# Moving the left-over weights of a mixture-of-experts router into the branch that uses them

## The chip, the cores and the metric

The kernel runs on one core of one Trainium2 chip. Its time is the device time of one execution in microseconds (us); below it is given as the median of several runs. The engines are PE (TensorE: matrix products), DVE (VectorE), ACT (ScalarE), POOL (GpSimd) and SP (SyncE, which here issues DMAs). A letter q behind an engine's name means its instruction sequencer: DMA issues, register loads, branches and semaphore waits. All times inside an execution are counted from its first instruction.

## What is computed

A decoder layer over 512 tokens and 16 meta tokens: attention and a state-space mixer in parallel, a gated merge, and then the part that the change touches, a hierarchical mixture of experts with 4 groups of 8 experts each.

```python
def hier_moe(v, w_group, b_group, w_expert, b_expert, w_gate, w_up, w_down):
    vt = v.reshape(-1, D_MODEL)                       # 512(+16) tokens x 1024
    g_logits = (vt @ w_group + b_group)
    p_group = jax.nn.softmax(g_logits, axis=-1)
    g_idx = jnp.argmax(g_logits, axis=-1)             # one group of 4
    p_g = jnp.take_along_axis(p_group, g_idx[:, None], axis=-1)
    e_logits = (vt @ w_expert + b_expert).reshape(-1, 4, 8)
    e_logits = jnp.take_along_axis(e_logits, g_idx[:, None, None], axis=1)[:, 0]
    top_vals, top_idx = lax.top_k(e_logits, 2)        # two experts of that group
    w = jax.nn.softmax(top_vals, axis=-1) * p_g
    ...
    for gi in range(N_EXPERT_GROUPS):                 # 32 experts, 1024 -> 256 -> 1024
        h = silu(einsum('td,edf->tef', vt, w_gate[sl])) * einsum('td,edf->tef', vt, w_up[sl])
        out = out + einsum('tef,te,efd->td', h, comb[:, sl], w_down[sl])
    return out.reshape(shp)
```

All is float32. The weights of the 32 experts are 3 MiB each: a gate and up table of 2 MiB (`gu`) and a down table of 1 MiB (`dn`).

## The kernel before

**Tokens and slots.** The 512 tokens are four blocks of 128 (b = 0 to 3). The kernel computes only chosen pairs: each expert has 64 slots (`CAP`), and a chosen token gets a slot by its rank among the tokens of that expert. A pass p of the expert loop takes two experts at once, 16 passes in all. A token whose rank is 64 or more, or whose group holds more than 256 tokens (`GCAP`), is left over: a general path (`tc.If(over > 0)`, line 1461) recomputes it with loops over all experts. The flag `ovi` is whether any expert has more than 64 tokens.

**The router**, lines 1354 to 1406, is written out by hand. PE follows the written order from line 1354 on; ACT, DVE and POOL follow it from line 1371 (`in_order`); the other engines' work and what stands outside is placed by a list scheduler at build time. For each block: `turn(b, hh)` adds the last projection to the residual, turns it on PE, sums its squares on ACT (`sqv`) and writes it to the DRAM table `vd`. `norm_v(b)` makes the factor of the norm (`ms` on DVE, a power on POOL) and writes it as a last column of `vd`. `logits` gives the router's products. `choose` is a generator of DVE steps (maximum, its index, the group's mask, the two best experts, the one-hot table `ohc`), cut up by `steps`. `rank` counts on PE, in the PSUM tile `rk`, how many earlier tokens chose the same expert; ACT copies the groups' ranks out (`rkg`, `rkf`). `find_slots` turns ranks to one-hot slot tables (`rr`). `weigh_exp` and `weigh` make the two weights, by an exponential on ACT. `place(b0, dst, v)` multiplies `rr` with the token numbers (v = 2, to `tb`) or with the weight table `vw` (v = 3, to `tw`): what comes out is, for every slot, its token or its weight. `idx` is `tb` as integers.

**What follows the router.** Three gathers on POOL (line 1431) fetch the rows of passes 0 to 2 from `vd` by `idx` into the tiles `xg`, which ACT has filled with zeros before (line 1422). Behind the gathers POOL sets `flag`, SP writes it to DRAM as `fence` (128 values of 4 bytes, line 1444), and only behind that issue SP loads the two halves of expert 4's `gu` (line 1445). `overflow` (line 1332) is for each of three block ranges 12 small steps on POOL that end in `wrest`, the weights of left-over tokens, and give `gk`, `bad` and `fine`, which the group tables need too. They too are placed behind the gathers. Then every engine loads `ovi` (line 1460) and branches around the general path (line 1461). Behind the branch SP issues the `dn` of experts 5 and 6 (line 1518) and then, in the expert loop, each next table as its buffer comes free: 7 `gu` buffers, 7 `dn` buffers.

**The expert loop**, from line 1696, keeps ACT, DVE, PE, POOL and SP in the written order: `turn_x` (turn the gathered rows on PE, `xT` on DVE), `expert_gu` (32 products, line 1554), activation, `expert_h`, the products with `dn` (line 1593), `combine` back to tokens, and a scatter of the finished rows after each group. `group_tables` (line 1633) runs on DVE once, in pass 0.

In these lines the order of the first steps is fixed:

```python
        norm_v(3)
        weigh(0)
        logits(3, 1)
        place(0, tb, 2)
        steps(c3, 10)
```

Of the kernel before, what the change touches and what calls it, by code (L numbers as in the profile page):

```python
# [73 lines left out]
def hybrid_layer(ctx: ExitStack, tc, A, out):  # L74
# [1052 lines left out]
    wrest = cp.tile([128, NE, 4], F32, name="wrest")  # L1127
# [7 lines left out]
    gk, bad, fine = (cp.tile([128, 4], F32, name=x) for x in ("gk", "bad", "fine"))  # L1135
# [14 lines left out]
    last_rs, last_sq = [None], [None]  # L1150

    def turn(b, hh, po=None):

        h = h2[:, b, hh * 512:(hh + 1) * 512]
        t = vT[b, hh] = gt("vbT", n=T, p=gr)
        pt = ps("pvT")
        two = b == 3 and hh
        for i in range(2):
            c = slice(i * 256, (i + 1) * 256)
            if po is not None and (two or i == 0):  # L1160
                o = c if two else slice(0, 512)
                dve.scalar_tensor_tensor(h[:, o], po[:, o], 0.5, h[:, o], op0=ALU.mult, op1=ALU.add)
            for k in (2 * i, 2 * i + 1):
                pe.transpose(pt[:, k * 128:(k + 1) * 128], h[:, k * 128:(k + 1) * 128], ident)
        last_sq[0] = act.activation(gt("sqv", n=T, p=gr), h, AF.Square, scale=2 * D ** -0.5, accum_out=vq[:, 2 * b + hh:2 * b + hh + 1])
        nc.sync.dma_start(vd[b * 128:(b + 1) * 128, hh * 512:(hh + 1) * 512], h)
        if two:
            return lambda: [dve.tensor_copy(t[:, i * 256:(i + 1) * 256], pt[:, i * 256:(i + 1) * 256]) for i in range(2)]
        elif hh:
            dve.tensor_copy(t, pt)  # L1170
        else:
            act.activation(t, pt, AF.Copy)
# [16 lines left out]
    def norm_v(b):  # L1189

        rs = vq[:, 8 + b:9 + b]
        t = sm.tile([128, 1], F32, tag="sq1", name="ms4", bufs=4)
        dve.tensor_scalar(t, vq[:, 2 * b:2 * b + 1], vq[:, 2 * b + 1:2 * b + 2], 4 * EPS, op0=ALU.add, op1=ALU.add)
        pool.tensor_tensor(rs, t, mhalf[:, :1], op=ALU.pow)
        q = nc.scalar if b < 3 else nc.sync
        last_rs[0] = q.dma_start(vd[b * 128:(b + 1) * 128, D:D + 1], rs)
# [3 lines left out]
    def choose(b0, b1):  # L1200
# [23 lines left out]
        vt_, vw, rr = rtile([2, 32]), rtile([4, 32]).rearrange("p b (k v) e -> p b k v e", k=2), rtile([2, 64])  # L1224
# [41 lines left out]
        chosen[b0] = b1, ak, vt_, vw, rtile([2]), rt_, rtile([2]), rr, rtile([2]), mx8, lg, gm, [rtile(n) for n in ([5], [5], [], [1], [1], [4])]  # L1266
# [10 lines left out]
    def weigh(b0):  # L1277

        b1, ak, vt_, vw, wk, rt_, rkk, rr, wx, mx8, lg, gm, (gd, eg, sg_, pg, e2, _) = chosen[b0]
# [52 lines left out]
    def overflow(b0):  # L1332

        b1, ak, vt_, vw, wk, rt_, rkk, rr, wx = chosen[b0][:9]
        g4_ = chosen[b0][12][5]
        pool.tensor_tensor(g4_, ohc[:, b0:b1, 32:], rkg[:, b0:b1], op=ALU.mult)
        pool.tensor_tensor(g4_[:, :, :2], g4_[:, :, :2], g4_[:, :, 2:], op=ALU.add)
        pool.tensor_tensor(gk[:, b0:b1], g4_[:, :, 0], g4_[:, :, 1], op=ALU.add)
        bd_ = bad[:, b0:b1]
        pool.tensor_scalar(wx, rkk, CAP - 0.5, None, op0=ALU.is_gt)  # L1340
        pool.tensor_scalar(bd_, gk[:, b0:b1], GCAP - 0.5, None, op0=ALU.is_gt)
        pool.tensor_tensor(bd_, bd_, wx[:, :, 0], op=ALU.add)
        pool.tensor_tensor(bd_, bd_, wx[:, :, 1], op=ALU.add)
        pool.tensor_scalar(fine[:, b0:b1], bd_, 0.5, None, op0=ALU.is_lt)
        pool.tensor_scalar(bd_, bd_, 0.5, None, op0=ALU.is_gt)
        pool.tensor_tensor(wx, wk, bd_[:, :, None].to_broadcast([128, b1 - b0, 2]), op=ALU.mult)
        pool.tensor_tensor(rt_, ak, wx[:, :, :, None].to_broadcast([128, b1 - b0, 2, 32]), op=ALU.mult)
        pool.tensor_tensor(wrest.rearrange("p e b -> p b e")[:, b0:b1], rt_[:, :, 0], rt_[:, :, 1], op=ALU.add)  # L1348
# [5 lines left out]
    with in_order(pe):  # L1354
# [18 lines left out]
        weigh_exp(0)  # L1373
        copies = turn(3, 1, po3)
        steps(c2)
        rank(2)
        copies()
        norm_v(3)
        weigh(0)
        logits(3, 1)  # L1380
        place(0, tb, 2)
        steps(c3, 10)
        weigh_exp(2)
        steps(c3)
# [9 lines left out]
        ovf, ovi = sm.tile([128, 1], F32, tag="sq1", name="ovf", bufs=4), cp.tile([128, 1], I32, name="ovi")  # L1394
        dve.tensor_reduce(ovf, rk[:, 144:176], axis=AX.X, op=ALU.max)
        dve.tensor_scalar(ovi, ovf, CAP + 0.5, None, op0=ALU.is_gt)
# [12 lines left out]

    n_traced = len(nc.cur_bb.bb.instructions)  # L1410
    overflow(0)
    overflow(2)
    overflow(3)
    overs = nc.cur_bb.bb.instructions[n_traced:]
# [216 lines left out]
    fst = cp.tile([128, 16], F32, name="fst")  # L1631

    def group_tables():
        goh = ohc[:, :, 32:]
        dve.tensor_scalar(fst, lpos, FIRST, None, op0=ALU.is_ge)
# [3 lines left out]
        dve.scalar_tensor_tensor(gtab[:, :, 0], goh, ic[:, 104:105], fine[:, :, None].to_broadcast([128, 4, 4]),  # L1639
# [250 lines left out]
```

## Time and profile before

| what | value |
|---|---|
| median of 3 runs | 827.81 us (826.03 to 828.17) |
| the profiled execution: its time | 824.92 us |
| its span, first to last instruction | 823.2 us |
| PE busy | 774.9 us, 94% |
| DVE, ACT, POOL busy | 454.9, 299.6, 147.5 us |
| moved by DMA | 163.39 MB, mean 198 GB/s |

The profiled execution is one of its own, 2.89 us under the median of the timed runs; what is added up inside it is counted against 824.92 us. PE's busy time counts pipelined products one by one, so 94% does not say that PE is at its limit. The page's row of DMA rates by slices is at about 420 GB/s from soon after the expert loop's start to near the end of the span, and at half of that or less in most slices before.

### The profile page before, as it was taken

To read this page: it belongs to the slowest core of one execution; us is meant where nothing else is said; L and a number is where in the kernel's file an instruction comes from. 1 tells how busy PE (TensorE), PEld (TensorE's weight loads), DVE (VectorE), ACT (ScalarE), POOL (GpSimd) and SP (SyncE) were. 2 spreads that over 40 slices of the span, in tenths; PEclk is the share of its full clock that TensorE was granted. 3 is DMA by queue.
4 is the path that set the end of the run, shared out by engine and by line. 5 is a ranking of instruction groups with operands and counts; after the bars stand their busy time and mean duration, and the time that the engine had idled before them with its cause. 6 is when DMAs were issued, how large, how long until landed. Compare 5 with 4: busy or idle time off the path is not lost.

```text
span 823.2 us, 11366 instructions
## 1 busy us (share of the span) xinstructions
PE 774.9 (94%) x4202; PEld 530.7 (64%) x4202; DVE 454.9 (55%) x1009; ACT 299.6 (36%) x564; POOL 147.5 (18%) x233
## 2 busy tenths in 40 slices
PE   4999999999999999999999899995699999999995
PEld 3999987677778878876666588884234343434342
DVE  3697528976356445477775775425243454543523
ACT  6455425333124374155554333412022322322313
POOL 5000103333112000023444300005300020200101
PEclk9999999999999999999999999997799999999998
DMA  7322226233231224021122595586799999999991
GB/s 254 109 61 97 103 67 203 92 126 129 78 111 56 103 86 155 14 62 31 44 53 66 159 423 194 175 333 204 153 422 421 419 418 420 417 420 418 420 386 40
DMA packets 40366, 163.39 MB, mean 198 GB/s; under 512 B 9152, under 2 KB 13648, under 8 KB 24176
## 3 DMA queue, kind: packets, MB, share of 16 engines
q1 hardware_dynamic: 35504, 154.46, 50.0%
q0 software_dynamic: 3984, 7.94, 3.0%
q8 instruction: 35, 0.57, 0.3%
q10 hardware_dynamic: 816, 0.20, 0.1%
q14 instruction: 27, 0.22, 0.1%
HBM read 159.30 MB, written 6.36 MB: 201 GB/s over the span
## 4 chain that ended last, share of the span: by engine, by line
PE 77%; DMA 8%; issue 5%; DVE 5%; ACT 3%; POOL 2%; POOLq 0%; SPq 0%; DVEq 0%; ACTq 0%
PE gu L1554 9%; DMA gu<-in_moe_gu_dram 5%; PE y L1593 5%; PE pbr L669 3%; PE pbr L672 3%; PE pbr L670 3%; PE pc L1620 2%; PE po L872 2%; PE ga L242 2%; PE gs L242 2%; PE ga L244 2%; PE ga L243 2%; PE gs L243 2%; PE gs L244 2%; PE pout L1094 2%
## 5 line engine op out<-in xcount | busy, mean ns | idle before, releaser
L1554 PE MATMUL gu<-gu,xT 128*64 128x512 f32 (+1 forms) x544 | 117.1, 576 | 5.5 <-DVE xT L1532 3.2
L1554 PEld LDWEIGHTS gu<-gu,xT 128*64 128x64 f32 x544 | 39.9, 139 | 80.0 <-issue 64.8
L1593 PE MATMUL y<-dn,hT 128*64 128x512 f32 x256 | 58.7, 599 | 0.3 <-ACT hT L1570 0.3
L1431 POOL DMA_INDIRECT xg<-vd,idx x16 | 16.3, 1021 | 165.8 <-DVE yl L1606 106.2
L1558 DVE SCALAR_TENSOR_TENSOR hp<-th,gu 128x256 f32<-128x256 f32 (+1 forms) x17 | 6.9, 404 | 68.7 <-ACT th L1557 68.6
L818 DVE CUSTOM_DVE_ANT_0 sp<-sp,amask 128x144 f32<-128x144 f32 (+4 forms) x80 | 33.9, 459 | 18.0 <-PE sp L810 16.0
L1557 ACT ACTIVATE th<-gu,rsl 128x256 f32<-128x256 f32 (+1 forms) x17 | 7.9, 462 | 98.8 <-PE gu L1554 98.8
L1604 ACT ACTIVATE yh<-xg 128x512 fp32r<-128x512 f32 x30 | 18.9, 630 | 57.8 <-DVE xg L1603 57.8
L1603 DVE SCALAR_TENSOR_TENSOR xg<-y,wsl,xg 128x512 f32<-128x512 f32 (+1 forms) x34 | 24.2, 717 | 27.4 <-PE y L1593 27.4
L1593 PEld LDWEIGHTS y<-dn,hT 128*64 128x64 f32 x256 | 16.9, 136 | 32.9 <-issue 31.7
L1606 DVE TENSOR_TENSOR yl<-xg,yh 128x512 fp32r<-128x512 f32 x30 | 20.8, 692 | 20.9 <-ACT yh L1604 20.9
L848 PE MATMUL st<-qs,kq 97*128 97x512 f32 (+4 forms) x80 | 28.6, 358 | 1.0 <-DVE kq L793 1.0
L1620 PE MATMUL pc<-yh,st 128*128 128x512 f32 x60 | 26.3, 439 | 0.0
L1530 PEld LDWEIGHTS pxT<-cst,xg 128*128 128x128 f32 x128 | 14.4, 146 | 17.5 <-issue 17.5
L1532 DVE TENSOR_TENSOR xT<-pxT,pv 128x512 f32<-128x512 f32 x32 | 20.5, 682 | 9.4 <-POOL wrest L1348 9.4
L302 POOL TENSOR_TENSOR rfs<-rfm,mhalf 128x4 f32<-128x4 f32 (+1 forms) x5 | 7.6, 1521 | 92.6 <-DVE rfm L301 92.6
L878 POOL TENSOR_TENSOR pw<-pw 128x400 f32<-128x400 f32 x14 | 15.9, 1157 | 44.3 <-PE po L872 44.3
L849 PE MATMUL st<-qs,kq 97*128 97x512 f32 (+4 forms) x80 | 23.6, 295 | 0.2 <-DMA qs<-rs 0.2
L857 ACT ACTIVATE pw<-st 128x512 f32<-128x512 f32 (+1 forms) x32 | 16.7, 547 | 19.3 <-PE st L853 16.1
L1620 PE MATMUL pc<-yl,st 128*128 128x512 f32 x60 | 23.7, 395 | 0.0
L1530 PE MATMUL pxT<-cst,xg 128*128 128x128 f32 x128 | 18.3, 289 | 5.3 <-DVEq L1461 5.3
L388 DVE SCALAR_TENSOR_TENSOR cacc<-xp,cwh,cacc 128x528 f32<-128x528 f32 x30 | 22.9, 764 | 0.4
(930 smaller groups left out, 2120.2 us busy)
## 6 DMA issues: line engine op xcount, KB each, us to landing
gu<-in_moe_gu_dram SPq DMA_DIRECT2D x64, 1024.0 KB, 20.5
dn<-in_moe_dn_dram SPq DMA_DIRECT2D x30, 1024.0 KB, 21.1
win<-in_win_dram SPq DMA_DIRECT2D x19, 1024.0 KB, 4.8
lm<-acd SPq DMA_DIRECT2D x16, 256.0 KB, 3.6
wbs<-in_wbs_dram SPq DMA_DIRECT2D x4, 1024.0 KB, 4.8
wba<-in_wba_dram SPq DMA_DIRECT2D x4, 1024.0 KB, 10.5
wo<-in_wout_dram SPq DMA_DIRECT2D x4, 1024.0 KB
ce<-acd SPq DMA_DIRECT2D x16, 128.0 KB, 7.2
```

Source lines behind the costliest of these rows:

```text
L242: pe.matmul(dst, ah, bh, start=(i == 0), stop=False)
L243: pe.matmul(dst, ah, bl, start=False, stop=False)
L244: pe.matmul(dst, al, bh, start=False, stop=(i == n - 1))
L669: pe.matmul(pb_, wh[:, k], oh[k], start=(k == 0), stop=False)
L670: pe.matmul(pb_, wh[:, k], ol[k], start=False, stop=False)
L672: pe.matmul(pb_, wl[:, k], oh[k], start=False, stop=(k == last))
L818: dve.tensor_tensor_reduce(s_, s_, amask[:, L - nk + n0:L - nk + n1], 1.0, -3.0e38, op0=ALU.add, op1=ALU.max, accum_out=mx[:, n_:n_ + 1])
L848: pe.matmul(d_, kh_[0:97, kb], qh_[0:97, q0:q1], start=True, stop=False)
L1530: pe.transpose(pt[:, k * 128:(k + 1) * 128], xgs[p % NX][:, (hh * 4 + k) * 128:(hh * 4 + k + 1) * 128], ident)
L1554: pe.matmul(gu[f][r, :2 * n], xT[p][:, k, r], w, start=(k == 0), stop=(k == KD - 1), skip_group_check=True)
L1593: pe.matmul(yp[hh][e * 64:(e + 1) * 64], hT_[p][:, f, e * 64:(e + 1) * 64], dns[(2 * p + e) % ND][:, f, hh * 512:(hh + 1) * 512], start=(f ...
L1620: pe.matmul(sums[b, hh], st[:, b * 128:(b + 1) * 128], x[:, c], start=(n == 0 and p % 4 == 0), stop=(n == 1 and p % 4 == 3), skip_group_ch ...
```

## The change

- `overflow` and its three calls go. The test of left-over tokens becomes `left_out`, 5 DVE steps over all four blocks at once. It is run twice: inside the general path, where the weights `wrest` are now made too, and at the head of `group_tables`, where `bad` is turned to 1 - `bad` in one more step.
- The weight table `vw` is no tile of its own any more: it lies, as `vws`, in columns of the constants tile `cst` whose constants have been read for the last time (four tables of 128 columns), for all four blocks.
- The count of tokens per expert, four products, goes from columns 144 to 176 of `rk` to a PSUM bank of its own, `cnt`, and on PE from before `place(2, tb, 2)` to behind it.
- The order of the router's steps: block 3's copies, `norm_v(3)` and `logits(3, 1)` come before the end of block 2's choice; `weigh_exp(0)` comes behind `norm_v(3)`; `place(0, tw, 3)` comes before `place(3, tb, 2)`; `ovf` and `ovi` come before `weigh(2)`.
- The norm's factor of block 3 is written to `vd` from ACT's queue, as the other blocks' are, and no longer from SP's. The zero fills of `xg` stand behind that issue. The load of `dn` 4 stands behind the last write of rows to `vd`, no longer behind the factor's.
- `lpos` and `wsl` are read out of PSUM by ACT instead of DVE.

```diff
-    wrest = cp.tile([128, NE, 4], F32, name="wrest")
...
-    gk, bad, fine = (cp.tile([128, 4], F32, name=x) for x in ("gk", "bad", "fine"))
+    rkc = cp.tile([128, 4, 2], F32, name="rkc")
+    vws = cst[:, CST["tri"][0]:CST["before"][1]].rearrange("p (b k v e) -> p b k v e", b=4, k=2, v=2)
...
-        last_sq[0] = act.activation(gt("sqv", n=T, p=gr), h, AF.Square, scale=2 * D ** -0.5, accum_out=vq[:, 2 * b + hh:2 * b + hh + 1])
-        nc.sync.dma_start(vd[b * 128:(b + 1) * 128, hh * 512:(hh + 1) * 512], h)
+        act.activation(gt("sqv", n=T, p=gr), h, AF.Square, scale=2 * D ** -0.5, accum_out=vq[:, 2 * b + hh:2 * b + hh + 1])
+        last_vd[0] = nc.sync.dma_start(vd[b * 128:(b + 1) * 128, hh * 512:(hh + 1) * 512], h)
...
-        q = nc.scalar if b < 3 else nc.sync
-        last_rs[0] = q.dma_start(vd[b * 128:(b + 1) * 128, D:D + 1], rs)
+        last_rs[0] = nc.scalar.dma_start(vd[b * 128:(b + 1) * 128, D:D + 1], rs)
...
-        vt_, vw, rr = rtile([2, 32]), rtile([4, 32]).rearrange("p b (k v) e -> p b k v e", k=2), rtile([2, 64])
+        vt_, vw, rr = rtile([2, 32]), vws[:, b0:b1], rtile([2, 64])
...
-    def overflow(b0):
...
+    def left_out(gk, bad):
+
+        g4_, w2 = sm.tile([128, 4, 4], F32, tag="g4_", name="g4_", bufs=1), sm.tile([128, 4, 2], F32, tag="w2", name="w2", bufs=1)
+        dve.tensor_mul(g4_, ohc[:, :, 32:], rkg)
+        dve.tensor_reduce(gk, g4_, axis=AX.X, op=ALU.add)
+        dve.tensor_scalar(w2, rkc, CAP - 0.5, None, op0=ALU.is_gt)
+        dve.tensor_tensor(w2[:, :, 0], w2[:, :, 0], w2[:, :, 1], op=ALU.max)
+        dve.scalar_tensor_tensor(bad, gk, GCAP - 0.5, w2[:, :, 0], op0=ALU.is_gt, op1=ALU.max)
...
         find_slots(0)
-        weigh_exp(0)
         copies = turn(3, 1, po3)
-        steps(c2)
-        rank(2)
+        steps(c2, 3)
         copies()
         norm_v(3)
+        weigh_exp(0)
+        steps(c2)
+        logits(3, 1)
+        rank(2)
         weigh(0)
-        logits(3, 1)
         place(0, tb, 2)
+        weigh_exp(2)
         steps(c3, 10)
-        weigh_exp(2)
         steps(c3)
         find_slots(2)
         rank(3)
+        place(2, tb, 2)
+        cnt = ps("cnt")
         for b in range(4):
-            pe.matmul(rk[:, 144:176], onesb, oh12s[b][:, :32], start=(b == 0), stop=(b == 3), skip_group_check=True)
-        place(2, tb, 2)
+            pe.matmul(cnt[:, :32], onesb, oh12s[b][:, :32], start=(b == 0), stop=(b == 3))
+        place(0, tw, 3)
         find_slots(3)
         weigh_exp(3)
         place(3, tb, 2)
+        ovf, ovi = sm.tile([128, 1], F32, tag="sq1", name="ovf", bufs=4), cp.tile([128, 1], I32, name="ovi")
+        dve.tensor_reduce(ovf, cnt[:, :32], axis=AX.X, op=ALU.max)
+        dve.tensor_scalar(ovi, ovf, CAP + 0.5, None, op0=ALU.is_gt)
         weigh(2)
...
         weigh(3)
-        for b in (0, 2, 3):
-            place(b, tw, 3)
-        dve.tensor_scalar(wsl, tw[:, :16], 2.0, None, op0=ALU.mult)
-        dve.tensor_copy(lpos, tw[:, 16:32])
+        place(2, tw, 3)
+        place(3, tw, 3)
+        act.activation(lpos, tw[:, 16:32], AF.Copy)
+        act.activation(wsl, tw[:, :16], AF.Copy, scale=2.0)
...
-    overflow(0)
-    overflow(2)
-    overflow(3)
...
-        tc.add_manual_dep(act.activation(x, ident[:, 0:1].to_broadcast([128, D + 1]), AF.Copy, scale=0.0).ins, last_sq[0].ins.name,
+        tc.add_manual_dep(act.activation(x, ident[:, 0:1].to_broadcast([128, D + 1]), AF.Copy, scale=0.0).ins, last_rs[0].ins.name,
...
-    with tc.issue_after(last_rs[0].ins):
+    with tc.issue_after(last_vd[0].ins):
...
     with tc.If(over > 0), tc.tile_pool(name="fb", bufs=1, side="right") as fb:
         wrd = drp.tile([NE, 128, 4], F32, name="wrd")
+        gk_, bad = fb.tile([128, 4], F32, tag="gk_", name="gk_"), fb.tile([128, 4], F32, tag="bad", name="bad")
+        left_out(gk_, bad)
+        wrest, wv = (fb.tile([128, n], F32, tag=x, name=x) for x, n in (("wrest", NE * 4), ("wv", NE)))
+        wrest = wrest.rearrange("p (e b) -> p e b", b=4)
+        for b in range(4):
+            dve.tensor_add(wv, vws[:, b, 0, 0], vws[:, b, 1, 0])
+            dve.tensor_scalar(wrest[:, :, b], wv, bad[:, b:b + 1], None, op0=ALU.mult)
...
     def group_tables():
         goh = ohc[:, :, 32:]
+        left_out(gk, bad)
+        dve.tensor_scalar(bad, bad, -1.0, 1.0, op0=ALU.mult, op1=ALU.add)
```

## Rows read from the trace of the kernel before

**Rows 1.** The end of the chain that ended last (start, duration, what).
```profile
781.31 19.86 DMA gu<-in_moe_gu_dram
```
**Rows 2.** Busy time by stretch: length, five engines, granted clock, DMA share, GB/s.
```profile
579.40:587.00 7.60, 4.36 (x15) 1.91 (x15) 3.02 (x12) 0.00 (x0) 3.89 (x21) 0.50 0.96 45
587.00:592.40 5.40, 5.40 (x24) 1.64 (x22) 0.00 (x0) 0.00 (x0) 0.00 (x0) 0.89 0.81 332
592.40:594.60 2.20, 1.73 (x12) 0.85 (x8) 0.74 (x2) 0.47 (x1) 0.00 (x0) 1.00 0.01 4
...
640.00:700.00 60.00, 59.48 (x286) 24.27 (x284) 26.43 (x53) 16.20 (x30) 7.44 (x9) 1.00 1.02 419
```
**Rows 3.** Timeline of SP's queue, 560 to 600 us.
```profile
566.24 0.33 SPq L1196 DMA_DIRECT2D vd<-vq  x1
566.62 0.42 SPq L1048 DMA_DIRECT2D dn<-in_moe_dn_dram  x1
577.88 0.34 SPq L1444 DMA_DIRECT2D fence<-flag  x1
578.39 4.00 SPq L1039 DMA_DIRECT2D gu<-in_moe_gu_dram  x2
593.68 0.95 SPq L1048 DMA_DIRECT2D dn<-in_moe_dn_dram  x2
```
**Rows 4.** Line 1461, the branch: instruction, count, ns, first and last start.
```profile
L1461 SPq EVENT_SEMAPHORE  x8: 17/17/17, 591.2 to 593.3; - x8
...
L1461 DVEq EVENT_SEMAPHORE  x1: 21/21/21, 578.6 to 578.6; - x1
```
**Rows 5.** DMA packets, MB, share of 16 engines: 579.4:587, 587:592.4, all queues in 551.5:554.5.
```profile
q1 hardware_dynamic: 41, 0.34, 93.4%
...
q1 hardware_dynamic: 244, 1.75, 79.1%
...
DMA packets 306, 1.25 MB, mean 415 GB/s; under 512 B 154, under 2 KB 154, under 8 KB 154
```
**Rows 6.** Timeline of all engines from the last gather to pass 0.
```profile
575.56 0.99 POOL L1431 DMA_INDIRECT xg<-vd,idx  x1 [0.30 <-issue]
...
577.76 0.09 POOL L1439 MEMSET flag<- 128x1 f32 x1
...
583.20 1.29 DVE L1532 TENSOR_TENSOR xT<-pxT,pv 128x512 f32<-128x512 f32 x2 [9.39 <-POOL wrest L1348]
583.95 9.16 PE L1554 MATMUL gu<-gu,xT 128*64 128x512 f32 x32 [3.24 <-DVE xT L1532]
...
593.83 0.42 DVE L1558 SCALAR_TENSOR_TENSOR hp<-th,gu 128x256 f32<-128x256 f32 x1 [7.57 <-ACT th L1557]
```
**Rows 7.** Timeline of all engines in the router's last steps, 561.5 to 573 us.
```profile
562.81 0.20 POOL L1273 TENSOR_TENSOR ru<-ru 128x8 f32<-128x8 f32 x1
...
562.98 0.74 DVE L1168 COPY vbT<-pvT 128x256 f32<-128x256 f32 x2
...
563.20 0.21 ACT L1275 ACTIVATE ru<-ru 128x10 f32<-128x10 f32 x1 [3.57 <-POOL ru L1274]
...
563.92 1.04 ACT L1422 ACTIVATE xg<-cst 128x1025 f32<-128x1025 f32 x1
...
564.58 1.04 PE L1329 MATMUL tb<-ru 128*64 128x16 f32 x16
...
564.76 0.16 DVE L1284 TENSOR_TENSOR ru<-ru 128x2 f32<-128x2 f32 x1
...
565.65 0.57 POOL L1194 TENSOR_TENSOR vq<-ms,mhalf 128x1 f32<-128x1 f32 x1
...
566.25 0.26 DVE L1232 SCALAR_TENSOR_TENSOR ru<-plg,vq,wrt 128x40 f32<-128x40 f32 x1 [1.32 <-POOL vq L1194]
...
571.74 0.16 DVE L1400 TENSOR_SCALAR idx<-tb 128x16 int32<-128x16 f32 x1
```
**Rows 8.** Timeline of ACT's queue: block 1's factor, written the way block 3's is now.
```profile
548.48 0.33 ACTq L1196 DMA_DIRECT2D vd<-vq  x1
```

More of the change, by code (lines that the diff above doesn't have):

```diff
@@ L1148, in out_half @@
         return po
-    last_rs, last_sq = [None], [None]
+    last_rs, last_vd = [None], [None]
     def turn(b, hh, po=None):
@@ L1265, in choose @@
             oh12s.append(ohc[:, b0 + b])
-        chosen[b0] = b1, ak, vt_, vw, rtile([2]), rt_, rtile([2]), rr, rtile([2]), mx8, lg, gm, [rtile(n) for n in ([5], [5], [], [1], [1], [4])]
+        chosen[b0] = b1, ak, vt_, vw, rtile([2]), rt_, rkc[:, b0:b1], rr, None, mx8, lg, gm, [rtile(n) for n in ([5], [5], [], [1])]
         yield
@@ L1277, in weigh @@
     def weigh(b0):
-        b1, ak, vt_, vw, wk, rt_, rkk, rr, wx, mx8, lg, gm, (gd, eg, sg_, pg, e2, _) = chosen[b0]
+        b1, ak, vt_, vw, wk, rt_, rkk, rr, wx, mx8, lg, gm, (gd, eg, sg_, pg) = chosen[b0]
         nb = b1 - b0
@@ L1330, in place @@
                               start=(b == 0 and k == 0), stop=(b == 3 and k == 1), skip_group_check=True)
-    def overflow(b0):
[L1334 to L1348, printed above, removed]
+    def left_out(gk, bad):
[5 more added lines that the diff above has]
+        dve.scalar_tensor_tensor(bad, gk, GCAP - 0.5, w2[:, :, 0], op0=ALU.is_gt, op1=ALU.max)
     def steps(g, n=99):
@@ L1392, in hybrid_layer @@
         place(3, tb, 2)
+        ovf, ovi = sm.tile([128, 1], F32, tag="sq1", name="ovf", bufs=4), cp.tile([128, 1], I32, name="ovi")
+        dve.tensor_reduce(ovf, cnt[:, :32], axis=AX.X, op=ALU.max)
+        dve.tensor_scalar(ovi, ovf, CAP + 0.5, None, op0=ALU.is_gt)
         weigh(2)
-        ovf, ovi = sm.tile([128, 1], F32, tag="sq1", name="ovf", bufs=4), cp.tile([128, 1], I32, name="ovi")
-        dve.tensor_reduce(ovf, rk[:, 144:176], axis=AX.X, op=ALU.max)
-        dve.tensor_scalar(ovi, ovf, CAP + 0.5, None, op0=ALU.is_gt)
         lpos = cp.tile([128, 16], F32, name="lpos")
@@ L1401, in hybrid_layer @@
         weigh(3)
-        for b in (0, 2, 3):
-            place(b, tw, 3)
-        dve.tensor_scalar(wsl, tw[:, :16], 2.0, None, op0=ALU.mult)
-        dve.tensor_copy(lpos, tw[:, 16:32])
+        place(2, tw, 3)
+        place(3, tw, 3)
+        act.activation(lpos, tw[:, 16:32], AF.Copy)
+        act.activation(wsl, tw[:, :16], AF.Copy, scale=2.0)
         in_turn.close()
-    n_traced = len(nc.cur_bb.bb.instructions)
-    overflow(0)
-    overflow(2)
-    overflow(3)
-    overs = nc.cur_bb.bb.instructions[n_traced:]
     front.close()
@@ L1421, in hybrid_layer @@
     for x in xgs:
-        tc.add_manual_dep(act.activation(x, ident[:, 0:1].to_broadcast([128, D + 1]), AF.Copy, scale=0.0).ins, last_sq[0].ins.name,
-                          mybir.DependencyInfo(mybir.DependencyClass.NoSync, mybir.DependencyReason.DATA), reason="behind the squares")
+        tc.add_manual_dep(act.activation(x, ident[:, 0:1].to_broadcast([128, D + 1]), AF.Copy, scale=0.0).ins, last_rs[0].ins.name,
+                          mybir.DependencyInfo(mybir.DependencyClass.NoSync, mybir.DependencyReason.DATA), reason="behind the norm")
     load_gu(6)
-    with tc.issue_after(last_rs[0].ins):
+    with tc.issue_after(last_vd[0].ins):
         for i in range(3, ND):
@@ L1437, in hybrid_layer @@
         for p in range(NX):
-            first3 = gather(p)
+            gather(p)
         pool.memset(flag, 0.0)
-    for i in overs:
-        tc.add_manual_dep(i, first3.ins.name, mybir.DependencyInfo(mybir.DependencyClass.NoSync, mybir.DependencyReason.DATA),
-                          reason="behind the gathers")
     fence = drp.tile([128, 1], F32, name="fence")
@@ L1630, in hybrid_layer @@
     gw = cp.tile([128, 2, 2, 4], F32, name="gw")
-    fst = cp.tile([128, 16], F32, name="fst")
+    fst, gk, bad = (cp.tile([128, n], F32, name=x) for x, n in (("fst", 16), ("gk", 4), ("bad", 4)))
     def group_tables():
         goh = ohc[:, :, 32:]
+        left_out(gk, bad)
+        dve.tensor_scalar(bad, bad, -1.0, 1.0, op0=ALU.mult, op1=ALU.add)
         dve.tensor_scalar(fst, lpos, FIRST, None, op0=ALU.is_ge)
@@ L1638, in group_tables @@
             dve.tensor_scalar(rrg[:, b], iot, gk[:, b:b + 1], None, op0=ALU.is_equal)
-        dve.scalar_tensor_tensor(gtab[:, :, 0], goh, ic[:, 104:105], fine[:, :, None].to_broadcast([128, 4, 4]),
+        dve.scalar_tensor_tensor(gtab[:, :, 0], goh, ic[:, 104:105], bad[:, :, None].to_broadcast([128, 4, 4]),
                                  op0=ALU.mult, op1=ALU.mult)
```

## The prediction

> **What bounds the kernel now.** I read from the end backwards. The chain of waits ends in loads of expert tables: PE's last pass starts when a load that the chain counts for 19.86 us has landed [rows 1]. The busy times by stretch say how far back that reaches: through the expert loop the DMA engines are at 1.02 of their time and move 419 GB/s [rows 2]. So there the end is a sum of bytes over a rate, and only two things can move it: the bytes, which the change leaves alone, and the moment from which the loads run without a pause. That moment is on SP's queue. SP issues expert 4's table at 578.39, and its next load, the `dn` pair of experts 5 and 6, only at 593.68 [rows 3].
>
> Why so late? SP's semaphore waits at the branch end between 591.2 and 593.3 [rows 4]; in 592.4 to 594.6 the DMA engines move 4 GB/s [rows 2]. I read this as SP waiting, behind the branch, for expert 4's two halves to land. And those land late. From 579.4 to 587.0 the engines are 0.96 busy at 45 GB/s, then at 332 GB/s [rows 2]: 41 packets of the loads' queue took 16 x 7.6 x 0.934 = 114 us of engine time, 2.8 us each, while the next 244 took 16 x 5.4 x 0.791 = 68 us, 0.28 us each [rows 5]. A tenfold slower stretch of 8 us begins just behind the `fence`, 128 neighbouring values of 4 bytes, issued at 577.88 [rows 3]. So I read the chain as: `idx` (571.74), three gathers (the last 575.56 + 0.99), `flag` (577.76), `fence` (577.88), 8 us of slow packets, the two halves, and 593.68 [rows 3, 6, 7]. From the fence to the resumed loads it is 593.68 - 577.88 = 15.80 us, and I take it as fixed.
>
> The chain of waits itself would point elsewhere: DVE's first `xT` waits 9.39 us, until 583.20, for POOL's `wrest`, and PE's first pass starts at 583.95 [rows 6]. That is a visible stall, but not on the path of the loads.
>
> **The change part by part.** *Left-over steps out of POOL.* 36 POOL steps go (12 in each of three calls). Some of them were placed between the last gather's end, 576.55, and the setting of `flag` at 577.76 [rows 6]. Without them `flag` is set at about 576.6 and the fence issued at about 576.75: 1.1 us sooner. This is the first term, -1.1. The others delayed `xT`. Without them `xT` waits for the branch: DVE got past it at 578.6 [rows 4], and now comes to it about 0.8 us sooner, as it no longer waits for the last `place` to read `lpos` and `wsl`. With about 1.9 us from there to the first product (one half's transposes, the `xT` step's 0.65, handovers), pass 0 starts at about 579.7 and not 583.95: 4.2 us sooner for PE, and nothing for the loads, as the buffers that it frees are asked for only behind the `dn` pair. Where the stall goes: PE then waits for loads in later passes instead.
>
> *What is added.* `left_out` and its inversion are 6 DVE steps, by the 0.16 us of a small step [rows 7] about 1.1 us, in pass 0. Their cover is DVE's wait of 7.57 us before 593.83 [rows 6]; without it they would cost 1.1. The general path's own steps cost nothing where the branch is passed: no line of its body appears in the trace. `lpos` and `wsl` on ACT: two small steps, and ACT's next work is pass 0's activation, 20 us later. The table in `cst` and the count's own bank are the same steps at other addresses; the bank frees `find_slots(3)` on DVE from waiting for the count, which gains nothing as long as `idx` hangs on PE (next part).
>
> *The router's order.* It moves `idx`, the start of the path above. Before, block 3's choice began at 566.25, after 1.32 us of waiting for the power on POOL, which ended at 566.22 [rows 7]. Now the square is no longer behind the exponential, which had waited 3.57 us for POOL until 563.20 [rows 7]. The copies start about 0.7 sooner (three small steps go behind them): 562.3 + 0.74 for the copies, 0.2 for `ms`, 0.1 + 0.57 for the power gives 563.9; the two differences and the exponential, 562.81 to 563.41 before, take 0.6; the four steps of `weigh(0)` about 0.7 [rows 7]. Block 3's choice so begins at about 565.2, 1.05 sooner, and what is late next is the exponential, no longer the power. Against that stands `place(0, tw)`: 16 products now run on PE before `place(3, tb)`, on which `idx` hangs. The 16 products of `place(0, tb)` took 1.04 us [rows 7]. Gain and cost cancel: -1.05 + 1.04 = 0. Unknown is where the builder puts the zero fills, 1.04 us each [rows 7]. Before, one ran right behind the squares; if one gets between the issue of the factor's write and the exponential, `idx` comes 1.0 us later. If the 16 products hide behind DVE's steps, it is 0.7 sooner. So `idx` moves by -0.7 to +1.0. I take +0.1, near the middle and the case without a fill, since the exponential's input is there about when the issue ends. Sum: -1.1 + 0.1 = -1.0 us, with bounds -1.8 and -0.1.
>
> *Moved DMAs.* The factor's write goes from SP at 566.24 [rows 3] to ACT's queue at about 563.9; behind it there are only the exponential, the rank copies and the fills, of which none can start much earlier. `dn` 4, issued at 566.62 [rows 3], moves up to about 562, behind the last rows of `vd`. The gathers need the factor's write. Its price lies between nothing (landed by 571.9, when `idx` is done) and 4 us (a rival below); I take nothing. The Trainium skill ("DMA: Bandwidth & Descriptors", Issuing engines are not separate DMA queues) says that another issuing engine saves only the issue, as all run on the same 16 DMA engines; by it the write gains nothing over the bulk from its new queue. Rows of the change's other queue bear on it: block 1's factor, issued at 548.48 [rows 8], was still among the packets of 551.5 to 554.5 [rows 5], up to 6 us later: by that, 563.9 + 6 = 569.9, in time.
>
> **The rivals.** *Pass 0 is what the loads wait for* (16 in 100). Then the end moves by PE's 4.2 us, and up to 1.1 more, since pass 0 ran at half clock in part (granted 0.50 until 587 [rows 2]): -4.2 to -5.3. For it: pass 0's products end at 593.1, half a us before the `dn` pair. Against: the pair uses no buffer of pass 0, and is issued first.
>
> *The fence is not what slows the loads* (8 in 100). Then the 8 us belong to something that goes, such as the POOL steps that run beside them until 583. The two halves, 2.1 MB, would flow at 332 to 419 GB/s from about 578 and land at 584, SP would pass the branch by then, and the loads resume some 9 us sooner: -9. Against: the slow stretch lasts 4 us longer than the POOL steps. For it: block 1's factor, 128 values of 4 bytes too, went out in a stretch in which the loads kept the whole at 415 GB/s [rows 5]; but those values lie a row of `vd` apart, the fence's side by side. The Trainium skill ("DMA: Bandwidth & Descriptors", Anatomy of one DMA) gives a DMA a fixed 2.0 us plus its bytes over 436 GB/s; by it the fence would be over at 580, and the rest of the slow stretch would need another cause. The stretch lasted until 587.
>
> *The factor's write lands late* (12 in 100; it ends slower). On ACT's queue it is issued at 563.9 while `gu` 6 and now also `dn` 4 are in flight. Block 1's write took up to 6 us beside full loads [rows 5, 8]; as an upper bound I take twice that, 575.9. The gathers then start by up to 575.9 - 571.9 = 4.0 us later, and the end comes by up to 4.0 - 1.1 = 2.9 later. It decides once the write lands after 573.0, that is `idx` plus the 1.1 won.
>
> **How the numbers follow.** The forecast (64 in 100): -1.0 us, range -1.8 to -0.1. On the profiled execution 824.9 - 1.0 = 823.9; the timed median is 2.9 above the profiled one, so 827.8 - 1.0 = 826.8. Its own range is 826.0 to 827.7. The rivals give 823.6 (down to 822.5), 818.8, and up to 830.7. The range leaves out the fence rival's 8 in 100 and the upper half of the last one's: 822.5 to 829.3. A measurement of this kernel can tell 0.3%, 2.5 us, from no change: the forecast lies inside. Faster: the first two rivals, 0.24. Slower: the part of the last one above +2.5, with what a scatter of 1 us carries over the bound, 0.07. The same: the rest, 0.69.
>
> **What would show it.** Right: `flag` within 0.1 us of the third gather's end; the fence 0.1 to 1.8 us sooner; pass 0's products at about 579.7; about 8 slow us behind the fence, and 15 to 16.5 us from the fence to the `dn` pair; 420 GB/s from there on. `idx` later than 572.7 would show a fill before the exponential. Wrong: loads resumed more than 3 us sooner (then which rival is told by whether the slow stretch shrank or SP passed the branch before expert 4 landed), or a gather that starts over 1 us behind `idx`.

## The result, and the profile after

The changed kernel takes 820.42 us (median; 818.55 to 821.15) against 826.92 (825.54 to 828.17) of the kernel before in the same session: a ratio of 0.9927, 95% interval 0.9912 to 0.9942. It is about 6 us faster. The prediction was -1.0 us, with a range from 822.5 to 829.3 us; the measured time lies below that range. The profiled execution, the fastest of the four, took 818.55 us; its span is 816.8 us (823.2 before).

The end still hangs on the loads, as in [rows 1]. The end of the chain of waits of the changed kernel (start, duration, what):

```profile
774.80 19.94 DMA gu<-in_moe_gu_dram
...
794.79 3.67 PE gu L1546 x30
```

So the question is again when the loads began to run without a pause. SP's queue, which answers to [rows 3]:

```profile
576.22 0.97 SPq L1048 DMA_DIRECT2D dn<-in_moe_dn_dram  x2
577.23 2.37 SPq L1429 DMA_DIRECT2D fence<-flag  x1
579.65 7.88 SPq L1039 DMA_DIRECT2D gu<-in_moe_gu_dram  x6
```

The order is another one. Before: fence, expert 4's two halves, the branch, and only then the `dn` pair of experts 5 and 6. Now the pair goes ahead of the fence, 17.46 us earlier (576.22 for 593.68). The line of the branch, which answers to [rows 4], says why:

```profile
L1446 SPq EVENT_SEMAPHORE  x8: 17/17/17, 573.4 to 573.9; - x8
...
L1446 SPq COMPARE_BRANCH  x1: 50/50/50, 570.7 to 570.7; - x1
...
L1446 DVEq EVENT_SEMAPHORE  x1: 21/21/21, 575.6 to 575.6; - x1
...
L1446 PEldq EVENT_SEMAPHORE  x1: 51/51/51, 576.1 to 576.1; - x1
```

SP takes the branch at 570.7, before the fence. Its eight semaphore waits are over at 573.9, where before they ended at 593.3, behind expert 4's halves. None of its loads is in flight by then: from 571.5 to 573 the DMA engines move 5 GB/s. No line of the diff moves the branch on SP: the order of what stands outside the hand-written part is made by the list scheduler when the program is built.

The busy times by stretch (columns as in [rows 2]):

```profile
577.00:583.50 6.50, 6.50 (x27) 2.76 (x27) 3.93 (x18) 0.00 (x0) 0.00 (x0) 0.73 0.96 356
583.50:591.60 8.10, 7.27 (x46) 3.03 (x44) 3.09 (x8) 1.89 (x3) 0.00 (x0) 1.00 1.02 143
591.60:600.00 8.40, 8.40 (x44) 3.02 (x41) 2.67 (x8) 1.73 (x3) 0.99 (x1) 1.00 0.99 416
...
640.00:700.00 60.00, 59.38 (x290) 25.45 (x288) 26.69 (x57) 16.82 (x31) 7.18 (x8) 1.00 1.02 419
```

The slow stretch is still there, now from 583.5 to 591.6, at 143 GB/s with the engines 1.02 busy. But more was moved around it. The packets of all queues from 556 to 600 us, first of the kernel before:

```profile
DMA packets 2186, 8.61 MB, mean 196 GB/s; under 512 B 842, under 2 KB 842, under 8 KB 1292
```

and of the changed kernel:

```profile
DMA packets 2521, 11.30 MB, mean 257 GB/s; under 512 B 878, under 2 KB 878, under 8 KB 1290
```

That is 2.69 MB more at the start of a loop that moves 419 GB/s: 2.69 / 0.419 = 6.4 us, and the two spans differ by 823.2 - 816.8 = 6.4 us. The whole gain in span shows in this one row.

The timeline of all engines from the router's last steps to pass 0, which answers to [rows 6, 7]:

```profile
564.15 2.94 ACT L1410 ACTIVATE xg<-cst 128x1025 f32<-128x1025 f32 x3
...
564.76 0.26 DVE L1231 SCALAR_TENSOR_TENSOR ru<-plg,vq,wrt 128x40 f32<-128x40 f32 x1
...
570.82 0.17 DVE L1393 TENSOR_SCALAR idx<-tb 128x16 int32<-128x16 f32 x1 [0.38 <-PE tb L1328]
...
571.72 1.19 POOL L1419 DMA_INDIRECT xg<-vd,idx  x1 [0.84 <-DVE ru L1283]
...
574.53 0.99 POOL L1419 DMA_INDIRECT xg<-vd,idx  x1 [0.30 <-issue]
575.52 0.11 POOL L1427 MEMSET flag<- 128x1 f32 x1
...
576.43 1.57 PEld L1522 LDWEIGHTS pxT<-cst,xg 128*128 128x128 f32 x8 [3.89 <-DVEq L1446]
576.46 1.94 PE L1522 MATMUL pxT<-cst,xg 128*128 128x128 f32 x8 [3.78 <-DMA xg<-vd,idx]
...
578.34 8.12 PE L1546 MATMUL gu<-gu,xT 128*64 128x512 f32 x32
```

`flag` is set where the third gather ends, `idx` comes 0.92 us earlier than before, and pass 0's first products start at 578.34 instead of 583.95. They end at 586.46 instead of 593.11: pass 0 has moved by 6.65 us, about as much as the span, so these rows alone do not tell whether the span follows the loads or pass 0.

### The profile page after: what moved, and what is told of

It reads as the page before. It is cut to its first block, busy times and chain, and to the rows that moved or that the text cites. A ratio compares the mean times of both kernels' runs of the same rounds, so it can differ in the third digit from the quotient of the medians.

```text
span 816.8 us, 11335 instructions
## 1 busy us (share of the span) xinstructions
PE 773.5 (95%) x4202; PEld 530.7 (65%) x4202; DVE 453.8 (56%) x1013; ACT 299.6 (37%) x566; POOL 141.3 (17%) x197
## 4 chain that ended last, share of the span: by engine, by line
PE 78%; DMA 8%; DVE 6%; issue 4%; ACT 2%; POOL 1%; POOLq 0%; SPq 0%; DVEq 0%; ACTq 0%
PE gu L1546 9%; DMA gu<-in_moe_gu_dram 5%; PE y L1585 5%; PE pbr L669 3%; PE pbr L672 3%; PE pbr L670 3%; PE po L872 2%; PE pc L1612 2%; PE ga L242 2%; PE gs L242 2%; PE ga L244 2%; PE ga L243 2%; PE gs L243 2%; PE pout L1094 2%; PE gs L244 2%
## 5 line engine op out<-in xcount | busy, mean ns | idle before, releaser
L848 PE MATMUL st<-qs,kq 97*128 97x512 f32 (+4 forms) x80 | 28.7, 359 | 1.0 <-DVE kq L793 1.0
L849 PE MATMUL st<-qs,kq 97*128 97x512 f32 (+4 forms) x80 | 23.7, 296 | 0.2 <-DMA qs<-rs 0.2
L850 PE MATMUL st<-qs,kq 97*128 97x512 f32 (+4 forms) x80 | 23.0, 294 | 0.0
```

The lines of the kernel that those rows point to most:

```text
L848: pe.matmul(d_, kh_[0:97, kb], qh_[0:97, q0:q1], start=True, stop=False)
```

## The experiments

Theory O: the gain is the order on SP, branch before fence. Theory R: the gain is the reordered router, with an earlier `idx`, `flag` and pass 0. A second question is what makes the slow stretch, since it still costs the changed kernel 8.1 x (0.419 - 0.143) = 2.2 MB, some 5 us. Ratios are to the kernel before, timed beside each run. Two columns of the table are used throughout: MB moved from 556 to 600 us, and the end of pass 0's 32 `gu` products (their start plus duration).

| run | ratio (95%) | span | MB, 556 to 600 | pass 0 ends |
|---|---|---|---|---|
| before | 1 | 823.2 | 8.61 | 593.11 |
| after | 0.9927 (0.9912 to 0.9942) | 816.8 | 11.30 | 586.46 |
| after_branch_late | 0.998 (0.9971 to 0.999) | 821.4 | 9.38 | 587.05 |
| before_branch_early | 0.9974 (0.9963 to 0.9985) | 819.2 | 9.98 | 592.02 |
| leftout_alone | 0.9926 (0.9909 to 0.9943) | 819.2 | 10.65 | 589.45 |
| router_alone | 0.9984 (0.9975 to 0.9993) | 823.8 | 8.61 | 593.83 |
| after_fence1 | 0.9865 (0.9851 to 0.988) | 812.3 | 13.64 | 586.77 |
| after_nofence | 0.9864 (0.9848 to 0.9879) | 814.8 | 13.55 | 589.24 |
| after_fence_spread | 0.9861 (0.9842 to 0.9879) | 812.6 | 13.63 | 587.11 |
| after_fence_64 | 0.9867 (0.9848 to 0.9886) | 812.7 | 13.57 | 587.14 |
| after_ev_split | 0.9887 (0.9867 to 0.9907) | 812.3 | 14.44 | 586.78 |
| before_fence1 | 0.9941 (0.9926 to 0.9957) | 818.0 | 11.40 | 592.32 |
| leftout_fence1 | 0.9886 (0.9869 to 0.9903) | 813.9 | 12.91 | 588.33 |
| late_fence1 | 0.9909 (0.9894 to 0.9923) | 814.3 | 12.11 | 586.38 |

Spans and times within one row come from one profiled execution. The stage itself starts up to 2.7 us apart from one to the next (the last norm block's first step on DVE between 559.88 and 562.57), and a profiled execution can be the fastest or the slowest of its kernel, so small differences are read from the ratios.

**after_branch_late: the changed kernel with the old order on SP.** In the changed kernel, SP reads `ovi` and branches only behind expert 4's load.

```diff
...
-        load_gu(EV)
+        ev_load = load_gu(EV)
...
+    n_traced = len(nc.cur_bb.bb.instructions)
     over = nc.values_load(ovi[0:1, 0:1], min_val=0, max_val=1)
+    for i in nc.cur_bb.bb.instructions[n_traced:]:
+        if i.engine == nc.sync.engine:
+            tc.add_manual_dep(i, ev_load.ins.name, ...NoSync..., reason="behind the load")
```

> The changed kernel with one thing set back: on SP the branch of the general path stands behind the fence and expert 4's load again, as in the kernel before (in the changed kernel SP took the branch at 570.7 to 573.9, ahead of the fence at 577.2). Theory O (the gain comes from this order on SP, which nobody wrote: the semaphore waits at the branch's end no longer wait out expert 4's load): the fence goes right behind flag, at about 575.7, the branch's waits end some 15 us behind it, at about 591, and the loads resume there: 1 to 2.5 us below the kernel before, so 4 to 5 of the 6 us of gain are lost, ratio 0.997 to 0.9985. Theory R (the gain is the earlier flag, idx and pass 0 of the rewritten router): nothing is lost, ratio 0.992 to 0.994.

0.998: most of the gain is gone, by theory O. SP's queue and the line of the branch in this run:

```profile
575.94 0.33 SPq L1430 DMA_DIRECT2D fence<-flag  x1
576.48 0.89 SPq L1039 DMA_DIRECT2D gu<-in_moe_gu_dram  x2
591.89 0.95 SPq L1049 DMA_DIRECT2D dn<-in_moe_dn_dram  x2
```

```profile
L1451 SPq EVENT_SEMAPHORE  x8: 17/17/17, 589.6 to 591.2; - x8
```

From the fence to the `dn` pair it is 15.95 us, as the prediction took it from the kernel before (15.80). The change's other gains (`flag`, `idx`, and pass 0, which ends 6.06 us earlier than before) are all in this run and bring 1.8 us of span. So the span does not follow pass 0 here.

**before_branch_early: the kernel before with the new order on SP.** The fence and expert 4's load are put behind the branch.

```diff
-    fence = drp.tile([128, 1], F32, name="fence")
-    with tc.issue_after(nc.sync.dma_start(fence, flag).ins):
-        load_gu(EV)
...
+    branch = nc.cur_bb.bb.instructions[-1]
+    fence = drp.tile([128, 1], F32, name="fence")
+    fenced = nc.sync.dma_start(fence, flag)
+    tc.add_manual_dep(fenced.ins, branch.name, ...NoSync..., reason="behind the branch")
+    with tc.issue_after(fenced.ins):
+        load_gu(EV)
```

> The kernel before, with the fence and expert 4's load put behind the branch on SP and nothing else changed; the router's steps and the left-over weights on POOL stay as they were. Theory O: SP passes the branch before 577.9, the fence and expert 4's load go at their old times, and the down tables 5 and 6 go as soon as DVE, PE and POOL are past the branch (POOL last, as it works on the left-over weights until 583.4: about 584 to 588) instead of 593.7: 4 to 6 us faster, ratio 0.993 to 0.995. Theory R: the same time as before, ratio 0.999 to 1.001.

0.9974: the direction is theory O's, the size about half. SP's queue:

```profile
576.90 0.34 SPq L1514 DMA_DIRECT2D fence<-flag  x1
...
579.28 4.67 SPq L1048 DMA_DIRECT2D dn<-in_moe_dn_dram  x2
588.61 4.24 SPq L1039 DMA_DIRECT2D gu<-in_moe_gu_dram  x4
```

The first of the pair is 14 us earlier than before, but here it stands behind the fence's writes and shares the slow stretch with expert 4, and the next tables wait until 588.61 for pass 0's buffers: pass 0 is as late as before, since `xT` still waits for POOL's left-over steps. So the order alone is not all. The changed kernel also has the pair ahead of the fence, and pass 0 earlier.

**leftout_alone and router_alone: the change in two halves.** The first has `left_out` in the branch and the table in the constants, with the router's order, the factor's queue and the count's bank as before; the second is the rest, with `overflow` as before.

> The change without its reordering of the router: the left-over weights are worked out in the branch, the weight table lies in dead constants, and the order of the router's steps, the queue of the norm's factor and the place of the counts are as in the kernel before. As built, SP has the branch ahead of the fence, as in the changed kernel. Theory O (the order on SP, which follows from the branch no longer reading what POOL makes behind the gathers): most of the gain is here, 4 to 5 of 6 us, ratio 0.994 to 0.9955. Theory R (the reordered router is the gain): flag comes at most 1.1 us earlier and no more, ratio 0.9985 to 1.0.

> The rest of the change alone: the router's order, the reads by ACT, the norm's factor on ACT's queue, the counts in a bank of their own; the left-over weights are made on POOL as before and read by the branch. As built, SP has the fence and expert 4's load ahead of the branch, as in the kernel before. Theory O: idx some 0.6 to 0.9 us earlier and the chain behind it as long as before: ratio 0.9985 to 0.9995. Theory R: most of the gain, ratio 0.993 to 0.996.

leftout_alone has the whole gain by its ratio, 0.9926, a little more than expected; router_alone has 0.9984. The interval of the first leaves some 1.4 us either way: its profiled execution, whose stage starts 1.53 us later than the changed kernel's, shows 4.0 of the 6.4 us of span. SP's queue in the first:

```profile
567.83 13.07 SPq L1048 DMA_DIRECT2D dn<-in_moe_dn_dram  x3
580.95 0.42 SPq L1427 DMA_DIRECT2D fence<-flag  x1
```

and in the second:

```profile
578.05 0.34 SPq L1446 DMA_DIRECT2D fence<-flag  x1
...
594.33 0.95 SPq L1048 DMA_DIRECT2D dn<-in_moe_dn_dram  x2
```

The order on SP turns with the left-over weights (and the weight table that goes with them) and not with the router. Theory R falls. Why it turns is argued and not shown: with `overflow` gone the branch reads nothing that POOL makes behind the gathers, so it is ready before `flag` is.

**after_fence1: one value instead of 128.**

```diff
-    fence = drp.tile([128, 1], F32, name="fence")
-    with tc.issue_after(nc.sync.dma_start(fence, flag).ins):
+    fence = drp.tile([1, 1], F32, name="fence")
+    with tc.issue_after(nc.sync.dma_start(fence, flag[0:1, :]).ins):
```

> The changed kernel with a fence that writes one value of flag to DRAM where it wrote 128, each of 4 bytes, from 128 partitions. Theory W (the 128 small writes slow what is queued behind them: expert 4's load, at 143 GB/s in 583.5 to 591.6 where 419 is the rate of the loop): the slow stretch goes, about 2.2 MB more are moved by 592, some 5 us: ratio 0.986 to 0.988 of the kernel before. Theory G (the slow packets come of the gathers, of the branch's code being fetched, or of the loads' own destination): the stretch stays and the ratio is that of the changed kernel, 0.992 to 0.994.

0.9865, theory W. The stretch that moved 143 GB/s, by busy times and by the packets of the loads' queue (583.5 to 591.5 us; packets, MB, share of the 16 engines):

```profile
583.50:591.60 8.10, 7.27 (x46) 3.13 (x44) 2.78 (x8) 1.89 (x3) 0.00 (x0) 1.00 1.01 423
```

```profile
q1 hardware_dynamic: 465, 3.41, 101.5%
```

With 128 writes the same queue moved, in 583.5 to 591.6:

```profile
q1 hardware_dynamic: 175, 1.16, 102.5%
```

The engines were as busy in both, but a packet of the loads took 16 x 8.1 x 1.025 / 175 = 0.76 us with 128 writes, and 16 x 8.0 x 1.015 / 465 = 0.28 us with one. The writes come up in the queue just ahead of the slow stretch. The changed kernel from 582 to 583.5:

```profile
DMA packets 214, 0.61 MB, mean 410 GB/s; under 512 B 140, under 2 KB 140, under 8 KB 140
```

With one value there are 15 packets under 512 B in the same 1.5 us.

**after_nofence: no write at all.** Expert 4's load waits for the memset of `flag` by a semaphore.

```diff
-        pool.memset(flag, 0.0)
-    fence = drp.tile([128, 1], F32, name="fence")
-    with tc.issue_after(nc.sync.dma_start(fence, flag).ins):
-        load_gu(EV)
+        flagged = pool.memset(flag, 0.0)
+    n_traced = len(nc.cur_bb.bb.instructions)
+    load_gu(EV)
+    for i in nc.cur_bb.bb.instructions[n_traced:]:
+        tc.add_manual_dep(i, flagged.ins.name, ...Sync..., reason="behind the gathers")
```

> The changed kernel without the fence: expert 4's load waits for the memset of flag itself, through a semaphore, and the write to DRAM is gone. Theory W: the slow stretch is gone with the writes, and the load goes some 2.4 us earlier on SP than behind the fence's issue: ratio 0.985 to 0.988. Theory G: only the fence's issue on SP is saved, at most 2 us: ratio 0.990 to 0.993.

0.9864, the same as with one value. The stretch in this run:

```profile
583.50:591.60 8.10, 7.38 (x44) 2.91 (x40) 2.24 (x8) 0.80 (x3) 0.00 (x0) 0.98 1.01 424
```

**after_fence_spread and after_fence_64: 128 values, but apart.** `fence` is a table of 128 x 1024 (or 128 x 16) values, and its first column is written: 4 KB (64 bytes) from one value to the next.

```diff
-    fence = drp.tile([128, 1], F32, name="fence")
+    fence = drp.tile([128, 1024], F32, name="fence")[:, :1]
```

> The changed kernel with the fence's 128 values of 4 bytes written 4 KB apart in DRAM where they lay side by side. With one value the loads behind ran at 423 GB/s in 583.5 to 591.6, with 128 side by side at 143. Theory N (writes that lie side by side hold one another up, and the queue behind them): the slow stretch goes, ratio 0.986 to 0.988. Theory P (it is the number of small writes, wherever they go): the stretch stays, ratio 0.992 to 0.994.

> The changed kernel with the fence's 128 values 64 bytes apart in DRAM. At 4 bytes apart the loads behind them moved 143 GB/s in 583.5 to 591.6, at 4 KB apart 421 GB/s. Theory N1 (only writes into the same few bytes hold each other up): 420 GB/s and 0.986 to 0.988. Theory N2 (it is the same page or bank of DRAM, thousands of bytes): as slow as side by side, 0.992 to 0.994. Between the two: part of the stretch stays, 0.988 to 0.992.

0.9861 and 0.9867: as many writes, no slow stretch. First 4 KB apart, then 64 bytes:

```profile
583.50:591.60 8.10, 7.27 (x46) 3.12 (x44) 2.49 (x7) 1.89 (x3) 0.00 (x0) 1.00 1.02 421
```

```profile
583.50:591.60 8.10, 7.27 (x46) 3.13 (x44) 2.49 (x7) 1.89 (x3) 0.00 (x0) 1.00 1.01 424
```

In the run with 4 KB the small packets come up from 583.5 to 585 (141 under 512 B), and the engines move 405 GB/s meanwhile. So it is not their number. Only where the 4-byte values lie side by side do the loads behind them slow down; 64 bytes apart is enough.

**after_ev_split: half of expert 4's load ahead of the gathers.** On top of after_nofence, the first half is let go behind `dn` 4.

```diff
             if DN_AT[i] == "c":
                 load_dn(i)
+        load_gu(EV, (0,))
...
-    load_gu(EV)
+    load_gu(EV, (1,))
```

> The changed kernel without the fence, and with the first half of expert 4's load let go right behind down table 4 (it waits only for its buffer) while the second half waits for the memset of flag as in the run without the fence. In that run the transfers stood still from about 571 to 573 and moved 120 to 290 GB/s until 583.5. Theory H (that hole can take 1 MB, 2.5 us at 419 GB/s): up to 2.5 us below the run without the fence, ratio 0.983 to 0.986. Theory S (the half stands ahead of the gathers, which come late by as much as it takes, and pass 0 with them): no gain over the run without the fence, or 1 us lost, ratio 0.986 to 0.988.

0.9887: no gain, theory S, though just above its range and not for its reason alone. The gathers do take longer (from the first one to pass 0's first transpose 5.73 us, in after_fence1 4.72). But the hole is taken too (298 GB/s in 572 to 577, where after_fence1 has 129): 14.44 MB are moved by 600, the most of all runs, and the span is still only that of after_fence1, although this profiled execution was the fastest of its four (814.09 us, median 816.01). Why that median is 1.2 to 1.8 us above those of the four runs before it is not shown; the intervals of the ratios overlap. The loads are no longer what the end waits for. Two steps of the last chain in after_fence1:

```profile
783.55 3.58 PE y L1585 x16
787.13 6.91 PE gu L1546 x64
```

From 700 us on it holds no load; in after_ev_split neither. PE runs from pass to pass. In the runs of which this holds, the time from the end of pass 0's products to the end of the span is the same: 812.3 - 586.77 = 225.5 in after_fence1, 225.6 in after_nofence, 225.5 in after_fence_spread, 225.6 in after_fence_64, 225.5 in after_ev_split. In the changed kernel it is 816.8 - 586.46 = 230.3, and the 4.8 more are waits for loads.

**before_fence1: the kernel before with one value.**

> The kernel before with a fence of one value where it wrote 128 side by side; SP's order as before (fence, expert 4's load, branch). If the 128 writes are what slowed expert 4's load, its halves land some 5 to 6 us behind their issue and not 13 to 15, SP's waits at the branch end at about 585 to 586 and the loads resume there: some 7 us gained on the loads, and pass 0 (matmuls from about 584) may take over as what the end waits for: ratio 0.990 to 0.993. Rival (the slow packets of the kernel before come of something else, such as the branch's code): ratio 0.998 to 1.0.

0.9941, just outside the range. SP's queue, the branch, and pass 0:

```profile
577.39 0.30 SPq L1444 DMA_DIRECT2D fence<-flag  x1
577.87 0.83 SPq L1039 DMA_DIRECT2D gu<-in_moe_gu_dram  x2
586.78 0.96 SPq L1048 DMA_DIRECT2D dn<-in_moe_dn_dram  x2
```

```profile
L1461 SPq EVENT_SEMAPHORE  x8: 17/17/17, 584.5 to 586.4; - x8
```

```profile
583.46 8.86 PE L1554 MATMUL gu<-gu,xT 128*64 128x512 f32 x32 [3.43 <-DVE xT L1532]
```

The 15.8 us from the fence to the pair shrink to 9.39. 11.40 MB are moved by 600, by the loads' rate worth 2.79 / 0.419 = 6.7 us, but pass 0 ends at 592.32, and 592.32 + 225.6 = 817.9 (measured 818.0): here PE has taken over, the last chain holds no load behind 590 us, and 5.2 us of span are left.

**leftout_fence1: leftout_alone with one value.**

> The left-over weights in the branch (the run of that part alone) with the fence of one value; the router's order as in the kernel before. In the runs with a small or spread fence the chain of waits over the last 200 us holds TensorE alone and no load, so that the end now follows pass 0's start. Theory Q: the router's order, worth nothing while the loads were the bound, now counts with what it gives pass 0: in the run of the left-over weights alone the first transpose of pass 0 stands 17.6 us behind the last norm block's first copy, in the run with the rewritten router and one value 15.8 us: some 1.5 to 1.8 us slower than that run, ratio 0.988 to 0.989. Rival (the loads are the bound still, or pass 0's start is set by the gathers' transfers): same as that run, ratio 0.985 to 0.987.

0.9886, theory Q. Pass 0 ends at 588.33, and 225.6 later the span ends. Against after_fence1 the router's new order is worth 0.2% by the medians of the ratios, whose intervals overlap a little, and 1.6 us of span; as long as the loads were the bound no gain on top of the left-over weights could be seen (0.9926 for leftout_alone, 0.9927 for the whole change, each with 0.15 to 0.17% either way).

**late_fence1: the old order on SP with one value,** the edits of after_branch_late and after_fence1 together.

> The changed kernel with both: on SP the branch behind the fence and expert 4's load, as in the kernel before, and the fence of one value. Two bounds are to be told apart by it. Loads: with SP late the down tables go when expert 4's halves have landed, at about 584 to 585, so some 12 MB are moved in 556 to 600, between the changed kernel (11.30 MB, span 816.8) and its run with one value (13.64 MB, 812.3); at 419 GB/s that is a span of 816.8 - 0.7 / 0.419 = 815.1, ratio 0.989 to 0.991. TensorE: from the end of pass 0's gu matmuls the runs that wait for no load took 225.5 to 225.7 us to the end, and pass 0 starts here as in the changed kernel: 812.3 to 812.5, ratio 0.986 to 0.987, if the loads are early enough with this order too. If the order on SP cost what it cost with 128 writes, the ratio would be 0.992.

0.9909, by the loads (0.989 to 0.991 had been expected). SP's queue, and the last chain:

```profile
575.07 0.30 SPq L1430 DMA_DIRECT2D fence<-flag  x1
575.60 0.82 SPq L1039 DMA_DIRECT2D gu<-in_moe_gu_dram  x2
584.86 0.96 SPq L1049 DMA_DIRECT2D dn<-in_moe_dn_dram  x2
```

```profile
729.47 20.48 DMA dn<-in_moe_dn_dram
...
750.01 21.61 DMA gu<-in_moe_gu_dram
...
771.68 20.58 DMA gu<-in_moe_gu_dram
```

12.11 MB by 600 give 816.8 - 0.81 / 0.419 = 814.9 by the loads; measured 814.3. The same sum gives 821.4 for after_branch_late (measured 821.4), 820.0 for before_branch_early (819.2), 818.4 for leftout_alone (819.2) and 823.2 for router_alone (823.8). Each holds for the profiled execution from which its MB are read; that of before_branch_early was its fastest (820.96 us, median 823.23).

## Why the prediction was wrong

*The step that failed:* "From the fence to the resumed loads it is 593.68 - 577.88 = 15.80 us, and I take it as fixed." The time itself was read rightly and holds where the order on SP holds (15.95 in after_branch_late). But it was not fixed by the change. The prediction read that SP waits at the branch for expert 4's halves, and did not ask whether the branch would stay behind them. In its place the changed kernel has the branch ahead of the fence on SP and the `dn` pair 17.46 us earlier; leftout_alone has the same order and the whole gain, and with the old order forced (after_branch_late) 0.2% of the 0.7% is left. That the branch moved because it no longer reads the left-over weights made at POOL's tail is argued, as said above. None of the rivals had this, though the signs of being wrong name it ("SP passed the branch before expert 4 landed"). The prediction counted every instruction that was moved by hand and none that the build moves in answer.

*The terms of the sum* held within their bounds, but the path through them was no longer the one that counts. The first, -1.1 for `flag`: it now follows the third gather at once (575.52 for 575.52), where 1.21 us lay between before. The second, `idx` by -0.7 to +1.0 and taken at +0.1: measured -0.92, of which 0.24 is an earlier start of the stage (that first DVE step at 560.63 for 560.87), so -0.68, the lower bound; no fill stood ahead of the exponential, and the 16 moved products hid but for 0.38 us. Both together are -1.9 us; after_branch_late, which has both and the old order on SP, measured -0.2% (-0.1 to -0.3), 0.8 to 2.4 us, and router_alone, which has the second alone, -0.16% (-0.07 to -0.25), 0.6 to 2.1 us.

*Pass 0* was taken at 579.7 and came at 578.34. DVE got past the branch at 575.6, 3.0 us sooner than before, where 0.8 had been taken. What released the first transposes is open: the trace names the gathered rows for the matmul and the branch on DVE for its weight load.

*The slow stretch* was put down to the fence's neighbouring values, and that is now shown (after_fence1, after_nofence, after_fence_spread, after_fence_64). The rival "the fence is not what slows the loads" falls. The prediction had an estimate from the Trainium skill ("DMA: Bandwidth & Descriptors", Anatomy of one DMA), by which the fence would be over after some 2 us and the rest of the stretch need another cause. The section gives that fit for DMAs that GpSimd issues, and the fence is issued by SP. When its writes were over no row shows; in the kernel before, 144 packets of the loads' queue with next to no bytes lie within 1.5 us of its issue (577.9 to 579.4). What failed is the step to another cause: it is the loads behind the writes that are slow.

*"Pass 0 is what the loads wait for"* falls by after_branch_late, where pass 0 is 6.06 us earlier than before and the time is 0.2% shorter. In another form, "PE becomes the bound", it decides every version without the slow writes but late_fence1.

*The factor's write on ACT's queue* did no harm that the rows show: the first gather starts 0.73 us behind the end of `idx`, where it was 0.86 before (572.76 - 571.90).

## What to carry to other kernels

Where a scheduler places part of the program, an edit that removes an input of a branch or of any block with waits can move that block on a queue, as here on SP; look first at what is queued behind it, and compare the order of the built programs before summing up durations. When a stretch is bound by transfers, count the bytes that have been moved by a fixed moment: that one row gave the spans of the versions that the loads bound to within 1 us. In this kernel the fence to DRAM is better as one value, as none, or as values 64 bytes apart; the version with one value is 5 us faster than the change, and what then counts is how early the first pass starts.

## What was not expected of the hardware

128 writes of 4 bytes that lie side by side in DRAM slow the loads queued behind them for 8 us: the loads moved 143 GB/s with the DMA engines 1.02 busy (45 GB/s at 0.96 in the kernel before), against 421 to 424 GB/s with one value, with none, or with 128 values 64 bytes or 4 KB apart. What inside the memory or the DMA engines holds them up stays open. The issue of the write on SP took 2.37 us in the changed kernel and 0.34 us with one value, but the same 128 values took 0.34 us in the kernel before and 0.42 in leftout_alone, so their number does not explain it; what does is open.
